# One moving operand for the high and the low part in the first half of two MLPs

## The chip, the cores and the metric

One core of a Trainium2 chip. The metric is the time of one execution on the device in microseconds (us). Here and below TensorE is the matmul engine (PE, its weight loads PEld), VectorE is DVE, ScalarE is ACT, GpSimd is POOL, and SP is the engine that issues most DMAs.

## What is computed

A trunk of two layers over 256 tokens of 1024 features in float32. Layer 0 mixes tokens with differential attention, layer 1 with sparse attention (an indexer picks 64 keys for each query). Each layer ends with the MLP that this case is about:

```
def sq_relu_mlp(h, w1, w2):          # w1: 1024 x 4096, w2: 4096 x 1024
    u = jax.nn.relu(h @ w1)
    return (u * u) @ w2

x = x + mix
x = x + sq_relu_mlp(rms_norm(x, norm_mlp[i]), mlp_w1[i], mlp_w2[i])
```

## The kernel before, in words

**Two parts of each number.** TensorE takes its operands here as float32r, a shorter float32. To keep precision every operand is split: the high part is the value rounded to float32r, the low part the rest. A product a x b is then three products: high x high, high x low, low x high. `unit` loads 1 MB of weights by one DMA on SP's queue into a raw buffer (three of them) and splits it: ScalarE copies to `whi` (L141), VectorE subtracts to `wlo` (L142). There are four pairs of split buffers. Activations lie transposed (features on the partitions, tokens in the columns) as pairs of tiles `act`, each 128 partitions x 4 k-tiles x 256 tokens. `make_h` fills the pair for a norm's output from transposes of x on TensorE (L218, L222, L224).

**The MLP** runs over 8 blocks of 512 hidden columns. `up(b)`, the first half, needs two weight units. For each of four groups of 128 hidden columns (m) it goes over 8 k-tiles of 128 features, with three products of 256 columns each (L464 to L466): a 128 x 128 piece of the weights is the stationary operand, a k-tile of h with its 256 tokens the moving one. All 24 products of a group add up in one half of a PSUM bank, so two groups share a bank and a block takes two banks from the four named `wk`. `post` then evacuates two groups at once (512 columns): ScalarE relu (L471), VectorE the square (L472), ScalarE the square again, rounded to the high part (L475), VectorE the difference as the low part (L476). In block 0 the four groups take a bank each (two `acc`, two `wk`), go over the k-tiles in two turns, and are evacuated one by one. The second half of block b takes two weight units as well: u's pieces are stationary, the weights move in 512 columns, three products each (L146, L148, L150 in the helper `mm3`), added over all blocks in four `acc` banks; after the last block VectorE adds the result to x (L515).

**Order.** The program's order is: up(0), then for each b up(b + 1), the second half of b. The framework's scheduler places instructions on each engine's queue by their dependences and its own estimates, and puts in the waits; a tile is given its buffer when it is first written and gives it back after its last reader. Each engine runs its queue in order. Loads of weights wait for a raw buffer, splits for a pair of split buffers. Lists of pauses (`PAUSE`) order the attention parts by hand; nothing of them lies in the MLPs. `act` has eight buffers of one part each.

Of the kernel before, what the change touches and what calls it, by code (L numbers as in the profile page):

```python
# [9 lines left out]
F32 = mybir.dt.float32  # L10
# [14 lines left out]
# columns of the packed small parameters  # L25
C_NORM = 0            # mix0, mlp0, mix1, mlp1: 8 each
C_GT = 32             # gains after the transposes: diff q, diff k, dsa q, dsa k
C_SUB = 36
C_CQ = 37             # 2
C_ROPE = 40           # 5 x 16  # L30
C_INV = 120           # 8
C_ID = 128            # identity
C_LAM = 256           # q1, k1, q2, k2: 64 each
# [6 lines left out]
# products of the projections that pass before a stage beside them is issued (none if not here)  # L40
# [5 lines left out]
def trunk(ctx: ExitStack, tc: tile.TileContext, x_in, pos_in, pack_in, wf, out):  # L46
# [5 lines left out]
    act = E(tc.tile_pool(name="act", bufs=8))  # L52
# [34 lines left out]
    # products of zeros while the inputs come: the tensor engine's clock rises with use  # L87
# [70 lines left out]
    def rsqrt(ss, parts, shape, scon=None):  # L158
        """(ss * m + eps) ** -0.5 [* scon], parts: (index, m) with m a number or a column;
        a start from exp(-ln / 2) and one step of Newton's method"""  # L160
        v = tiny.tile(shape, F32, name="rs_v")
        y = tiny.tile(shape, F32, name="rs_y")
        a = tiny.tile(shape, F32, name="rs_a")
        r = tiny.tile(shape, F32, name="rs_r", bufs=6)
        with tc.issue_after(tables[0]):
            for i, m in parts:
                nc.vector.tensor_scalar(v[i], ss[i], m, EPS, op0=OP.mult, op1=OP.add)
                nc.scalar.activation(y[i], ss[i], AF.Ln, bias=eps[:, 0:1], scale=m)
            nc.scalar.activation(y, y, AF.Exp, scale=-0.5)
        nc.vector.tensor_tensor(a, y, y, op=OP.mult)  # L170
        nc.vector.scalar_tensor_tensor(a, a, -0.5, v, op0=OP.mult, op1=OP.mult)
        if scon is not None:
            nc.vector.tensor_tensor(y, y, scon, op=OP.mult)
        nc.vector.scalar_tensor_tensor(r, a, 1.5, y, op0=OP.add, op1=OP.mult)
        return r

    def rsqrt_start(v, shape):
        """v ** -0.5 from the exponent's half and three steps, without a table"""
        y = tiny.tile(shape, F32, name="rs_y")
        a = tiny.tile(shape, F32, name="rs_a")  # L180
        nc.vector.tensor_scalar(y.bitcast(I32), v.bitcast(I32), -0.5, float(0x5f3759df),
                                op0=OP.mult, op1=OP.add)
        for _ in range(3):
            nc.vector.tensor_tensor(a, y, y, op=OP.mult)
            nc.vector.scalar_tensor_tensor(a, a, -0.5, v, op0=OP.mult, op1=OP.mult)
            nc.vector.scalar_tensor_tensor(y, a, 1.5, y, op0=OP.add, op1=OP.mult)
        return y

    def row_scale(need_s):
        """mean square of x per token -> 1/(ms+eps) and its square root"""  # L190
        ss = tiny.tile([128, 2], F32, name="rowss")
        for t in range(2):
            j = sc.tile([128, D], F32, name="qn")
            with tc.issue_after(behind[0]):
                nc.scalar.activation(j, x[t], AF.Square, accum_out=ss[:, t:t + 1])
        v = tiny.tile([128, 2], F32, name="rowv")
        nc.vector.tensor_scalar(v, ss, 1.0 / D, EPS, op0=OP.mult, op1=OP.add)
        s2 = tiny.tile([128, 2], F32, name="rows2")
        nc.vector.reciprocal(s2, v)
        s = None  # L200
        if need_s:
            s = const.tile([128, 2], F32, name=f"srow{need_s}")
            nc.vector.tensor_copy(s, rsqrt_start(v, [128, 2]))
        return s, s2

    def new_h():
        return [[act.tile([128, 4, 256], F32R, name="act") for _ in range(2)] for _ in range(2)]
# [3 lines left out]
    def make_h(h, gc, t, n, js=(0, 1)):  # L211
        """columns of x, transposed, with the norm's gain, in two parts"""
        hi, lo = h[n]
# [12 lines left out]
    def lhs(h, kt, t):  # L226
        hi, lo = h[kt // 4]
# [3 lines left out]
    def project(ps, h, parts, n):  # L231
        """ps[t] = h[t] @ w; parts: (columns of a unit's two tiles, number of k-tiles)"""
# [19 lines left out]
    def rope_tables():  # L252
# [20 lines left out]
        # angles beyond 2^23: whole multiples of 2^24 are taken off and reduced by themselves  # L273
# [3 lines left out]
        # multiples of 2 pi, in two parts, times 2 pi in three: the products are exact but the last  # L277
# [11 lines left out]
        # the rest: multiples of 2^24 modulo 2 pi  # L289
# [33 lines left out]
    def rope(v, t, ty, ng, ns, eng):  # L323
        """v: [128, ng*ns, 64] in SBUF; group g has the gains of type ty+g"""
# [17 lines left out]
    def qk_post(ps, m, scon, ty, ng, nq, gcols, nm):  # L342
        """QK-norm, rotary and transposes of 8 heads' columns, ps[t]: [128, 512], the first nq of
        them queries. Keys are scaled here, queries' scales are left to the softmax.
        Returns two tiles [128, 2, 256] (two heads' dims on the partitions, tokens free), scales."""
# [33 lines left out]
    def dots(q, k):  # L379
        """products of two heads' queries and keys, on the two halves of the rows in turn"""  # L380
# [7 lines left out]
    def scores(qT, kT, i, mask):  # L388
        """masked scores of two heads, queries on partitions: columns 0..127 keys of the
        first token tile's queries, 128..383 of the second's. Keys come negated."""  # L390
# [10 lines left out]
    def expo(s, mn, nsc, z):  # L401
        """exp((score - max) * scale), nsc[:, t] = -scale"""
# [16 lines left out]
    def weighted(ps, c, w, aT, v, vc):  # L419
        """ps[:, c + t*w ...] = probabilities @ values"""  # L420
# [4 lines left out]
    def out_proj(o, us, h, gc, needs=((),) * 4):  # L425
        """x += o @ w_out, in four units of two k-tiles; h: the next norm's, transposed;
        needs[u]: the work beside that brings unit u's part of o"""
# [19 lines left out]
    def mlp(h, after):  # L447
# [4 lines left out]
        def up(b):  # L452
            u1 = [unit(pieces=4 if b < 2 else 2) for _ in range(2)]
            uh = act.tile([128, 4, 256], F32R, name="act")
            ul = act.tile([128, 4, 256], F32R, name="act")
# [3 lines left out]
            def group(ps, m, ks):  # L459
                wh, wl = w[m // 2]  # L460
                c = slice((m % 2) * 128, (m % 2) * 128 + 128)
                for k in ks:
                    hh, hl = h[k // 4][0][:, k % 4], h[k // 4][1][:, k % 4]
                    mm(ps, wh[:, k, c], hh, start=k == 0, stop=False)  # L464
                    mm(ps, wh[:, k, c], hl, start=False, stop=False)  # L465
                    mm(ps, wl[:, k, c], hh, start=False, stop=k == 7)  # L466

            def post(ps, m, cnt):
                r = sc.tile([128, 512], F32, name="sq")[:, :cnt * 256]
                q = sc.tile([128, 512], F32, name="on")[:, :cnt * 256]  # L470
                nc.scalar.activation(r, ps, AF.Relu)  # L471
                nc.vector.tensor_tensor(q, r, r, op=OP.mult)  # L472
                oh = uh[:, m:m + cnt].rearrange("p a b -> p (a b)")
                ol = ul[:, m:m + cnt].rearrange("p a b -> p (a b)")
                nc.scalar.activation(oh, r, AF.Square)  # L475
                nc.vector.tensor_tensor(ol, q, oh.bitcast(F32), op=OP.subtract)  # L476

            if b == 0:
                pss = [(acc() if m < 2 else wk())[:, :256] for m in range(4)]
# [3 lines left out]
                for m in range(4):  # L483
                    post(pss[m], m, 1)
            else:
                for mh in range(2):
                    ps = wk()
                    for m in range(2):
                        group(ps[:, m * 256:(m + 1) * 256], mh * 2 + m, range(8))
                    post(ps, mh * 2, 2)  # L490
# [28 lines left out]
    # ================= layer 0: differential attention =================  # L519
# [40 lines left out]
    def diff_probs(ps, res, nm):  # L560
        """unnormalized p1 - lam * p2 of two heads, keys on partitions, and 1 / sums"""
        qT, kT, rs = yield from qk_post(ps, s2c, scon, 0, 2, 4, (C_GT, C_GT + 1), nm)
        zs = tiny.tile([128, 2, 2, 2], F32, name="zs")       # head, component, token tile
# [77 lines left out]
    # ================= layer 1: sparse attention =================  # L641
# [6 lines left out]
    # compressed queries (their scale is left for later), index keys, index weights, index  # L648
    # queries, scores and the choice of the keys
    cqh = act.tile([128, 4, 256], F32R, name="act")  # L650
    cql = act.tile([128, 4, 256], F32R, name="act")
# [95 lines left out]
    # queries, keys, values  # L747
# [22 lines left out]
    def dsa_probs(half, out):  # L770
        """probabilities of eight heads, keys on partitions"""
# [53 lines left out]
def _tiles(w):  # L825
    """[k*128, n] -> [128, k*n]: each partition's k-tiles side by side"""
# [4 lines left out]
def _weights(i):  # L831
    """the weights in the order of their use, [128, columns] blocks one after another"""
# [44 lines left out]
def _pack(i):  # L877
    """small parameters, one column or one row for all partitions each"""
# [40 lines left out]
```

## Time and profile before

| | |
|---|---|
| three timed runs | 614.53 us median, 614.32 to 617.05 |
| profiled execution | span 611.9 us, 9330 instructions; the page gives no other time of it |
| TensorE, products | 597.8 us busy (98%), 3576 |
| TensorE, weight loads | 516.5 us busy (84%), 3576 |
| VectorE | 397.8 us busy (65%), 947 |
| ScalarE | 355.1 us busy (58%), 664 |
| GpSimd | 15.8 us busy (3%), 53 |
| DMA | 102.35 MB, mean 167 GB/s |

One execution was profiled, from the first instruction to the last (the span). A busy time counts each instruction from start to end, so products that overlap in the engine's pipeline count once in the share but have "mean ns" longer than the step from one start to the next; the steps are read from the timeline. "Idle before <-releaser" says what the engine had waited for. A few per cent of the products' records can be missing.

### The profile page before, as it was taken

The numbers are of one execution on the slowest core, as the hardware profiler recorded it, in microseconds if no ns is written. First come the engines' busy times: TensorE is split into PE (matmuls) and PEld (weight loads), VectorE is DVE, ScalarE is ACT, GpSimd is POOL, SyncE is SP. The second block draws the span as 40 slices with busy tenths as digits, with TensorE's granted clock in tenths as the row PEclk, the third lists the DMA queues.
The fourth block names the chain that finished last, engine by engine and source line by source line (L and its number), as shares of the span: only waits on it lengthen the run. The fifth ranks groups of instructions, "written<-read, shape, count | busy, mean of one in ns | idle before, by whom it ended". The sixth has DMA issues, their size and how long they took to land.

```text
span 611.9 us, 9330 instructions
## 1 busy us (share of the span) xinstructions
PE 597.8 (98%) x3576; PEld 516.5 (84%) x3576; DVE 397.8 (65%) x947; ACT 355.1 (58%) x664; POOL 15.8 (3%) x53
## 2 busy tenths in 40 slices
PE   8899999999999999999999899999999999999997
PEld 7677778899989989989887677778999899889986
DVE  5798986577465455456588999766755554564442
ACT  6788987676345345444387589784843453354330
POOL 5400000000000000000000000000000000000000
PEclk9899999999999999999999999999999999999999
DMA  8574343436545545554555226324465565555401
GB/s 312 186 259 154 138 174 127 176 114 227 182 177 205 199 159 193 207 179 153 203 163 182 69 70 207 139 69 138 160 224 177 198 206 168 185 199 197 148 2 69
DMA packets 16029, 102.35 MB, mean 167 GB/s; under 512 B 1904, under 2 KB 2416, under 8 KB 4336
## 3 DMA queue, kind: packets, MB, share of 16 engines
q1 hardware_dynamic: 15696, 101.62, 47.1%
q8 instruction: 28, 0.46, 0.3%
q10 hardware_dynamic: 288, 0.13, 0.1%
q14 instruction: 17, 0.14, 0.1%
HBM read 100.70 MB, written 1.05 MB: 166 GB/s over the span
## 4 chain that ended last, share of the span: by engine, by line
PE 80%; DVE 13%; ACT 2%; POOL 2%; issue 2%; DVEq 0%; POOLq 0%; ACTq 0%
PE acc L150 15%; PE acc L148 15%; PE acc L146 14%; PE wk L466 9%; PE wk L465 9%; PE wk L464 9%; DVE wlo L142 4%; DVE s L396 2%; PE wk L414 2%; PE wk L385 1%; PE wk L218 1%; DVE score L741 1%; DVE qkss L352 1%; ACT whi L141 1%; DVE m L740 1%
## 5 line engine op out<-in xcount | busy, mean ns | idle before, releaser
L142 DVE TENSOR_TENSOR wlo<-raw,whi 128x1024 fp32r<-128x1024 f32 (+2 forms) x210 | 229.8, 1116 | 167.9 <-ACT whi L141 167.8
L141 ACT ACTIVATE whi<-raw 128x1024 fp32r<-128x1024 f32 (+2 forms) x210 | 198.1, 973 | 185.3 <-PE acc L150 90.9
L146 PE MATMUL acc<-whi,act 128*128 128x512 f32 (+1 forms) x504 | 199.8, 397 | 2.0 <-ACT whi L141 2.0
L148 PE MATMUL acc<-wlo,act 128*128 128x512 f32 (+1 forms) x504 | 198.8, 394 | 0.8 <-DVE wlo L142 0.8
L150 PE MATMUL acc<-whi,act 128*128 128x512 f32 (+1 forms) x504 | 198.3, 394 | 0.0
L466 PE MATMUL wk<-act,wlo 128*128 128x256 f32 x480 | 135.9, 283 | 0.0
L465 PE MATMUL wk<-act,whi 128*128 128x256 f32 x480 | 135.9, 283 | 0.0
L464 PE MATMUL wk<-act,whi 128*128 128x256 f32 x480 | 135.8, 283 | 0.0
L146 PEld LDWEIGHTS acc<-whi,act 128*128 128x128 f32 x504 | 95.8, 190 | 21.3 <-ACT whi L141 2.4
L148 PEld LDWEIGHTS acc<-wlo,act 128*128 128x128 f32 x504 | 95.5, 190 | 19.9 <-DVE wlo L142 1.4
L150 PEld LDWEIGHTS acc<-whi,act 128*128 128x128 f32 x504 | 95.6, 190 | 18.9 <-issue 1.0
L464 PEld LDWEIGHTS wk<-act,whi 128*128 128x128 f32 x480 | 92.1, 192 | 0.5
L465 PEld LDWEIGHTS wk<-act,whi 128*128 128x128 f32 x480 | 92.1, 192 | 0.5
L466 PEld LDWEIGHTS wk<-act,wlo 128*128 128x128 f32 x480 | 92.1, 192 | 0.0
L407 ACT ACTIVATE s<-s,nb,rs_r 128x128 f32<-128x128 f32 x64 | 34.2, 537 | 8.0 <-DVE nb L405 8.0
L472 DVE TENSOR_TENSOR on<-sq 128x512 f32<-128x512 f32 (+1 forms) x36 | 22.4, 625 | 1.9 <-ACT sq L471 1.9
L222 ACT ACTIVATE act<-wk,pack 128x128 fp32r<-128x128 f32 x64 | 18.3, 374 | 8.6 <-PE wk L218 8.6
L476 DVE TENSOR_TENSOR act<-on,act 128x512 fp32r<-128x512 f32 (+1 forms) x36 | 22.3, 625 | 0.2
L475 ACT ACTIVATE act<-sq 128x512 fp32r<-128x512 f32 (+1 forms) x36 | 20.7, 574 | 0.1
L224 DVE SCALAR_TENSOR_TENSOR act<-wk,pack,act 128x128 fp32r<-128x128 f32 x64 | 18.0, 343 | 3.7 <-ACT act L222 3.6
L414 PE MATMUL wk<-pack,s 128*128 128x128 f32 x72 | 15.7, 290 | 2.3 <-DVE s L578 1.6
L471 ACT ACTIVATE sq<-wk 128x512 f32<-128x512 f32 (+1 forms) x32 | 17.7, 553 | 0.0
(178 smaller groups left out, 448.6 us busy)
## 6 DMA issues: line engine op xcount, KB each, us to landing
raw<-in_w SPq DMA_DIRECT2D x91, 1024.0 KB, 4.8
x<-in_x SPq DMA_DIRECT2D x4, 256.0 KB, 4.5
raw<-in_w SPq DMA_DIRECT2D x4, 256.0 KB, 5.2
raw<-in_w SPq DMA_DIRECT2D x2, 512.0 KB, 5.5
raw<-in_w SPq DMA_DIRECT2D x1, 984.0 KB, 5.6
raw<-in_w SPq DMA_DIRECT2D x1, 840.0 KB, 4.5
out_dram<-x SPq DMA_DIRECT2D x3, 256.0 KB, 2.0
out_dram<-x SPq DMA_DIRECT2D x2, 128.0 KB, 1.8
```

The lines of the kernel that those rows point to most:

```text
L141: nc.scalar.activation(hi[:, c], raw[:, c], AF.Copy)
L142: nc.vector.tensor_tensor(lo[:, c], raw[:, c], hi[:, c].bitcast(F32), op=OP.subtract)
L146: mm(ps, ah, wh, start=first, stop=False)
L148: mm(ps, ah, wl, start=False, stop=False)
L150: mm(ps, al, wh, start=False, stop=last)
L407: nc.scalar.activation(p[:, TS[t]], s[:, TS[t]], AF.Exp, bias=nb[:, t:t + 1], scale=nsc[:, t:t + 1], accum_out=z[t])
L414: nc.tensor.transpose(pt[:, i * 128:(i + 1) * 128], p[:, i * 128:(i + 1) * 128], ident)
L464: mm(ps, wh[:, k, c], hh, start=k == 0, stop=False)
L465: mm(ps, wh[:, k, c], hl, start=False, stop=False)
L466: mm(ps, wl[:, k, c], hh, start=False, stop=k == 7)
L472: nc.vector.tensor_tensor(q, r, r, op=OP.mult)
L476: nc.vector.tensor_tensor(ol, q, oh.bitcast(F32), op=OP.subtract)
```

## The change

The high and the low part of an activation become the two halves of one tile, and the first half of the MLPs uses them as one moving operand of 512 columns: the weights' high part meets both at once, the bank's first half collects high x high, its second half high x low, and the third product (low weights x high activations) is added to the second half. The evacuation therefore adds the two halves first, and is done for each group of 128 hidden columns by itself. The pool `act` has four buffers of twice the size. Everything else that the diff touches is text: comments are dropped, and other users of the pair take `parts()` or the first two of its three names.

```
-    act = E(tc.tile_pool(name="act", bufs=8))
+    act = E(tc.tile_pool(name="act", bufs=4))
...
+    def parts():
+        a = act.tile([128, 2, 4, 256], F32R, name="act")
+        return a[:, 0], a[:, 1], a
+
     def new_h():
-        return [[act.tile([128, 4, 256], F32R, name="act") for _ in range(2)] for _ in range(2)]
+        return [parts() for _ in range(2)]
...
         def up(b):
             u1 = [unit(pieces=4 if b < 2 else 2) for _ in range(2)]
-            uh = act.tile([128, 4, 256], F32R, name="act")
-            ul = act.tile([128, 4, 256], F32R, name="act")
+            uh, ul, _ = parts()
...
                 for k in ks:
-                    hh, hl = h[k // 4][0][:, k % 4], h[k // 4][1][:, k % 4]
-                    mm(ps, wh[:, k, c], hh, start=k == 0, stop=False)
-                    mm(ps, wh[:, k, c], hl, start=False, stop=False)
-                    mm(ps, wl[:, k, c], hh, start=False, stop=k == 7)
+                    hi, _, both = h[k // 4]
+                    mm(ps.rearrange("p (a b) -> p a b", b=256), wh[:, k, c], both[:, :, k % 4], start=k == 0, stop=False)
+                    mm(ps[:, 256:], wl[:, k, c], hi[:, k % 4], start=False, stop=k == 7)
 
-            def post(ps, m, cnt):
-                r = sc.tile([128, 512], F32, name="sq")[:, :cnt * 256]
-                q = sc.tile([128, 512], F32, name="on")[:, :cnt * 256]
-                nc.scalar.activation(r, ps, AF.Relu)
-                nc.vector.tensor_tensor(q, r, r, op=OP.mult)
-                oh = uh[:, m:m + cnt].rearrange("p a b -> p (a b)")
-                ol = ul[:, m:m + cnt].rearrange("p a b -> p (a b)")
-                nc.scalar.activation(oh, r, AF.Square)
-                nc.vector.tensor_tensor(ol, q, oh.bitcast(F32), op=OP.subtract)
+            def post(ps, m):
+                r = sc.tile([128, 256], F32, name="sq")
+                q = sc.tile([128, 256], F32, name="on")
+                nc.scalar.activation(r, ps[:, 256:], AF.Copy)
+                nc.vector.tensor_tensor(r, ps[:, :256], r, op=OP.add)
+                nc.vector.scalar_tensor_tensor(q, r, 0.0, r, op0=OP.max, op1=OP.mult)
+                nc.scalar.activation(uh[:, m], q, AF.Copy)
+                nc.vector.tensor_tensor(ul[:, m], q, uh[:, m].bitcast(F32), op=OP.subtract)
 
             if b == 0:
-                pss = [(acc() if m < 2 else wk())[:, :256] for m in range(4)]
+                pss = [(acc() if m < 2 else wk()) for m in range(4)]
...
-                    post(pss[m], m, 1)
+                    post(pss[m], m)
             else:
-                for mh in range(2):
+                for m in range(4):
                     ps = wk()
-                    for m in range(2):
-                        group(ps[:, m * 256:(m + 1) * 256], mh * 2 + m, range(8))
-                    post(ps, mh * 2, 2)
+                    group(ps, m, range(8))
+                    post(ps, m)
```

## Rows read from the trace of the kernel before

**Rows 1.** The page: busy time by engine; the chain that ended last.
```profile
PE 597.8 (98%) x3576; PEld 516.5 (84%) x3576; DVE 397.8 (65%) x947; ACT 355.1 (58%) x664; POOL 15.8 (3%) x53
...
PE 80%; DVE 13%; ACT 2%; POOL 2%; issue 2%; DVEq 0%; POOLq 0%; ACTq 0%
```
**Rows 2.** Windows: the two MLPs (start:end, length, busy by engine).
```profile
core 0: us, PE busy (x) PEld busy (x) DVE busy (x) ACT busy (x) POOL busy (x), PEclk, DMA share, GB/s
126.72:308.87 182.15, 182.15 (x1176) 166.27 (x1175) 102.93 (x135) 87.70 (x128) 0.00 (x0) 1.00 0.51 184
428.00:610.90 182.90, 180.21 (x1160) 164.71 (x1158) 95.79 (x119) 79.45 (x110) 0.00 (x0) 1.00 0.47 161
```
**Rows 3.** Waits, the longest in total, of the engines and of SP's queue.
```profile
engine line waited for: us in total, times, longest us
DVE wlo L142 <- ACT whi L141: 167.8, 77, 3.7
ACT whi L141 <- PE acc L150: 90.9, 33, 3.5
ACT whi L141 <- PE wk L465: 87.7, 28, 3.6
...
SPq L135 <- DVE wlo L142: 470.8, 81, 14.7
```
**Rows 4.** Timeline of PE: first products of three blocks (start us, us).
```profile
240.58 0.40 PE L146 MATMUL acc<-whi,act 128*128 128x512 f32 x1
...
251.48 0.28 PE L464 MATMUL wk<-act,whi 128*128 128x256 f32 x1
251.60 0.28 PE L465 MATMUL wk<-act,whi 128*128 128x256 f32 x1
...
263.00 0.40 PE L146 MATMUL acc<-whi,act 128*128 128x512 f32 x1
```
**Rows 5.** Timeline of PE: first and last of 35 products of 328 columns.
```profile
311.38 0.31 PE L148 MATMUL acc<-wlo,act 128*128 128x328 f32 x1
...
316.50 0.31 PE L150 MATMUL acc<-whi,act 128*128 128x328 f32 x1
```
**Rows 6.** Timeline of PE: transposes between products.
```profile
303.49 0.39 PE L218 MATMUL wk<-pack,x 128*128 128x128 f32 x2
303.63 0.48 PE L148 MATMUL acc<-wlo,act 128*128 128x512 f32 x1
303.95 0.39 PE L150 MATMUL acc<-whi,act 128*128 128x512 f32 x1
```
**Rows 7.** Groups of VectorE by shape (busy us, mean ns, idle before).
```profile
L472 DVE TENSOR_TENSOR on<-sq 128x512 f32<-128x512 f32 x28 | 19.2, 684 | 0.0
L476 DVE TENSOR_TENSOR act<-on,act 128x512 fp32r<-128x512 f32 x28 | 19.1, 684 | 0.0
...
L443 DVE TENSOR_TENSOR x<-acc,x 128x256 f32<-128x256 f32 x16 | 5.8, 415 | 0.0
...
L578 DVE SCALAR_TENSOR_TENSOR s<-s,w 128x256 f32<-128x256 f32 x8 | 3.8, 478 | 0.0
...
L472 DVE TENSOR_TENSOR on<-sq 128x256 f32<-128x256 f32 x8 | 3.2, 420 | 1.9 <-ACT sq L471 1.9
L476 DVE TENSOR_TENSOR act<-on,act 128x256 fp32r<-128x256 f32 x8 | 3.2, 418 | 0.2
```
**Rows 8.** Groups of ScalarE by shape.
```profile
L222 ACT ACTIVATE act<-wk,pack 128x128 fp32r<-128x128 f32 x64 | 18.3, 374 | 8.6 <-PE wk L218 8.6
L475 ACT ACTIVATE act<-sq 128x512 fp32r<-128x512 f32 x28 | 17.4, 620 | 0.0
L471 ACT ACTIVATE sq<-wk 128x512 f32<-128x512 f32 x28 | 16.2, 579 | 0.0
...
L475 ACT ACTIVATE act<-sq 128x256 fp32r<-128x256 f32 x8 | 3.3, 412 | 0.1
...
L471 ACT ACTIVATE sq<-wk 128x256 f32<-128x256 f32 x4 | 1.5, 370 | 0.0
```
**Rows 9.** Windows: one period; inside a first-half block; inside a second-half block.
```profile
172.30:194.70 22.40, 22.40 (x146) 20.51 (x146) 11.84 (x12) 10.04 (x12) 0.00 (x0) 1.00 0.51 188
...
140.00:150.00 10.00, 10.00 (x86) 10.00 (x85) 7.87 (x12) 5.37 (x8) 0.00 (x0) 1.00 0.57 210
152.00:161.00 9.00, 9.00 (x41) 7.44 (x41) 5.92 (x6) 4.00 (x6) 0.00 (x0) 1.00 0.50 185
```
**Rows 10.** Timeline of DVE: the low part for the first second-half block.
```profile
141.96 2.35 DVE L142 TENSOR_TENSOR wlo<-raw,whi 128x1024 fp32r<-128x1024 f32 x2
```
**Rows 11.** Timeline of PE: where the first second-half block starts.
```profile
150.90 0.40 PE L146 MATMUL acc<-whi,act 128*128 128x512 f32 x1
151.13 0.40 PE L148 MATMUL acc<-wlo,act 128*128 128x512 f32 x1
```
**Rows 12.** Timeline of PE: the start of layer 0's MLP.
```profile
126.86 0.36 PE L464 MATMUL acc<-act,whi 128*128 128x256 f32 x1
127.06 0.28 PE L465 MATMUL acc<-act,whi 128*128 128x256 f32 x1
127.18 0.38 PE L218 MATMUL wk<-pack,x 128*128 128x128 f32 x2
```
**Rows 13.** Timeline of ACT in the same stretch.
```profile
127.46 2.67 ACT L222 ACTIVATE act<-wk,pack 128x128 fp32r<-128x128 f32 x10
```

More of the change, by code (lines that the diff above doesn't have):

```diff
@@ L204, in row_scale @@
         return s, s2
+    def parts():
+        a = act.tile([128, 2, 4, 256], F32R, name="act")
+        return a[:, 0], a[:, 1], a
     def new_h():
-        return [[act.tile([128, 4, 256], F32R, name="act") for _ in range(2)] for _ in range(2)]
+        return [parts() for _ in range(2)]
     behind = []
     def make_h(h, gc, t, n, js=(0, 1)):
-        hi, lo = h[n]
+        hi, lo, _ = h[n]
         for j in js:
@@ L226, in lhs @@
     def lhs(h, kt, t):
-        hi, lo = h[kt // 4]
+        hi, lo = h[kt // 4][:2]
         c = slice(t * 128, t * 128 + 128)
@@ L646, in trunk @@
             [(*uc[0], 6), (uc[1][0][:, :656], uc[1][1][:, :656], 2)], 328)
-    cqh = act.tile([128, 4, 256], F32R, name="act")
-    cql = act.tile([128, 4, 256], F32R, name="act")
+    cqh, cql, _ = parts()
     cq = [(cqh, cql)]
```

## The prediction

> **What bounds the kernel now.** I read the page first: TensorE is busy 98% of the span and the chain that ended last is 80% TensorE [rows 1]. A busy TensorE need not run at its peak, since its ends are modelled, so I went on to the stretches of the two MLPs. In each, TensorE is busy for all or nearly all of some 182 us at a granted clock of 1.00, its higher level of 2.4 GHz, while VectorE and ScalarE are busy about half of it [rows 2]. The list of waits agrees: its long entries are VectorE waiting for ScalarE's halves of the weights, ScalarE waiting for TensorE to give weight buffers back, and the queue of weight loads waiting for VectorE to free raw buffers [rows 3]. All of them wait, by one or two steps, for TensorE. So an MLP lasts as long as its products take to start one behind another, and the change is worth what it does to those starts.
>
> The timeline gives them. One first-half block (`up` of one b) starts at 251.48 and the second-half products behind it at 263.00: 11.52 us for 96 products of 256 columns, 120.0 ns each. The second-half block before it, 240.58 to 251.48, is 48 products of 512 columns: 227.1 ns each [rows 4]. The difference, 107.1 ns for 256 columns, is 0.418 ns a column, one column per cycle at 2.4 GHz. What is left is 12.9 ns at either width. A third width tests this: the 328-column products start 34 times between 311.38 and 316.50, 150.6 ns apart [rows 5], where 12.9 + 328 x 0.418 gives 150.0. So a product costs its columns and a fixed 13 ns or so, and its weight load lies beside the product ahead of it.
>
> **The change, part by part.** The columns stay: per k-tile and 128 hidden columns 3 x 256 before, 512 + 256 after. One product in three goes, with its weight load: 4 (m) x 8 (k) x 16 (blocks, two layers) = 512 of them. A block has 32 x (227.1 + 120.0) = 11.11 us instead of 11.52, and 16 blocks save 16 x 0.41 = **6.6 us**. All of it is on the path, as nothing else ends later there [rows 2].
>
> That the 512-column product keeps the price of the present one is a choice. Its moving operand is in two runs of 256 columns, 1024 elements apart, which no product before has. Lower end: 13 ns a product lower, as if even its fixed part were hidden, 6.6 us more gain. Upper end: a break in the operand costs what the change from a transpose to a product costs. There a 512-column product holds the engine for 320 ns (303.63 to 303.95) instead of 227, so 93 ns more [rows 6]; 512 x 93 = 47.6 us, a net loss of 41. I take no extra cost: the nearest row is the plain product of the same width, and one third of the products before change to another place in the same tensors at each step without losing the line.
>
> The evacuation grows. Per block before, VectorE has two products and two differences of 512 columns, 4 x 0.684 = 2.74 us; after, four times an addition from PSUM (0.415, as the residual's addition), a maximum-and-product (0.478, as the same form on 256 columns in SBUF) and a difference (0.418): 5.24 us [rows 7]. ScalarE goes from 2 x (0.579 + 0.620) = 2.40 us to 4 x (0.370 + 0.412) = 3.13 us [rows 8]. In one period of 22.40 us (one block of each half) VectorE has 11.84 us of work now and ScalarE 10.04 [rows 9]; after, some 14.3 and 10.8 of 22.0. Cost: nothing, hidden by TensorE. Its cover is this: what a block evacuates is first used a second-half block later, 10.9 us on, and the chain of five operations takes 2.1 us. Behind these operations in VectorE's and ScalarE's queues wait the splits of the weights, and behind those, by raw buffers, the weight DMAs on SP's queue. Where the two engines are fullest, at the start of an MLP, the low part of the weights for the first second-half block is split by 144.31 [rows 10] and its first reader, the second product of that block, starts at 151.13 [rows 11]: 6.8 us to spare. The first block's evacuation adds 5.24 - 4 x (0.420 + 0.418) = 1.9 us and half of the second's 1.3 us more. Over 3 us remain. If that cover were gone, the loss would be the overhang, once per layer.
>
> PSUM: a later block now takes four banks (one per m) instead of two. Four are there and the same bank comes round a period later, so no wait. The four banks of the first block are as many as before.
>
> The merged tile of high and low part is one buffer of four in place of two of eight; what is alive at once (h, two hidden blocks; o and h) is the same number of bytes, and pairs were freed within one product of each other. Cost nothing. One new wait is possible at the start of each MLP. There the first products (126.86) start while the last transposes of x are still to be evacuated [rows 12, 13]: already the tile in use is being written in other columns. The joint read spans from the high to the low part. If that is taken as one stretch, the first product waits for the tile's last high part, the second piece of the group that starts at 127.46, so until about 128.2 (pieces of 0.37, some 0.27 apart). Five products of 120 ns that now run between the transposes come later: 0.6 us a layer, 1.2 in all. Lower end 0: only what is read is waited for. I take 0.3. Queued behind it on TensorE are the remaining transposes, on which the rest of h waits.
>
> **Sum.** Profiled span 611.9 - 6.6 + 0.3 = 605.6 us. The page gives no time of that execution beyond its span; the median of the timed runs is 614.5, 2.6 more, for what lies around it. That stays: **608.2 us**.
>
> At one place a page speaks against the size. The Trainium skill (TensorE: Matmul & The Clock Gate, Back-to-back issue gap) has a warm product cost its columns at 2.4 GHz plus 2.5 ns, not 13. By that 512 products fewer save 1.3 us, an estimate from that page, and the time would be 613.2. The rows give 120.0 ns for 256 columns where the page's form gives 109, so the measurement decides on the size of the fixed part. That all of it goes with the instruction no row shows.
>
> **The rivals.**
> 1. The fixed part, or most of it, stays with the run of columns and not with the instruction: two runs in one product cost twice 12.9. For it: no operand in two runs is in the trace. Against: nothing in the rows speaks of runs. Gain nil, plus 0.3: 614.8. (The case of the page above is near it.)
> 2. Slower: the break in the moving operand stalls the array. Place: every 512-column product of the first half; from 12.9 ns a break on there is no gain, from 19 ns on (another 3.1 us) it is slower by over 0.5%. Priced by the switch row, 93 ns: 614.5 + 41 = 655. Against: rows 4 and 5 show the line of columns undisturbed by any change of address between products.
> 3. The weight loads pace the first half. For it: there PEld is busy 10.00 of 10.00 us, in the second half 7.44 of 9.00 [rows 9]. Then the remaining 256-column product, its load beside a 512-column one, would fall to its columns, 107.1 ns, and the pair to 334.2: 512 x (360 - 334.2) = 13.2 us, 601.3. Against: the 328- and 512-column products have the same 13 ns with their loads well hidden.
>
>    The Trainium skill (Perfetto Trace Analysis, Identifying the Most-Contended Engine) would have TensorE judged by this share of loads; the three widths on one line say otherwise here.
> 4. The gain is there, but about three us come back: the wait at the MLPs' start at its upper end (1.2), and a split that is late at the start of an MLP, held in its queue behind an evacuation that waits for its group of products. A group lasts 11.11 / 4 = 2.8 us and over 3 us are spare, so it takes two such holds; their overhang is some 1 us a layer. Against: the splits there are ahead of need by more than any one hold. 608.2 + 0.9 + 2 = 611.1.
>
> **How the numbers follow.** Forecast 0.70 (its own range 607 to 609.5), rival 4 0.13, rival 1 0.09, rival 2 0.05, rival 3 0.03. The range of 8 in 10 takes in the forecast and rival 4: 606.0 to 612.5. Half a per cent, about what a measurement of this kernel can tell from no change, is 3.1 us: faster means under 611.4. The forecast, rival 3 and some two thirds of rival 4 are there: 0.82. Rival 1 and the rest of rival 4 are within: 0.13. Rival 2 is slower: 0.05.
>
> **What would show it.** In a first-half block of the changed kernel, starts 227 and 120 ns apart in turn and 11.1 us from the first to the second half's next product; an MLP of some 179 us; 512 products and loads fewer; TensorE still without idle time in the MLPs; VectorE at 65% there. A step of 240 ns or more after the 512-column products would be rival 1 (above 246, rival 2), one of 107 after the others rival 3. Idle time of TensorE released by `wlo`, or by `act` at the start of an MLP, would be rival 4. The prediction is wrong if the steps are right and the time isn't: then the attention parts, which the diff leaves alone, have moved.

## The result and the profile after

Eight runs of each kernel: 612.0 us median (609.86 to 612.57) against 614.7 (614.22 to 617.27). The ratio of the changed kernel to the one before is 0.994, 95% interval 0.9922 to 0.9959, or 2.5 to 4.8 us less. The forecast was 608.2, 1.0% less. The direction held and so did the wide range; the likeliest case's own range, 607 to 609.5, did not. One run of the kernel before and one of `wides`, both in a later comparison, took 3.34 ms each; the ratios below are without them. The profiled execution's span is 609.2 us, 2.7 less than before.

The page of the changed kernel, its line of busy time by engine:

```profile
PE 595.2 (98%) x3064; PEld 490.0 (80%) x3064; DVE 428.7 (70%) x1067; ACT 368.5 (60%) x720; POOL 15.9 (3%) x53
```

512 products and 512 weight loads are gone, as worked out, VectorE and ScalarE are fuller, and TensorE is as busy as it was [rows 1]. The windows of the two MLPs and of one period, which answer to [rows 2, 9] (start:end, length, busy by engine, granted clock):

```profile
126.88:307.06 180.18, 180.18 (x920) 152.09 (x919) 118.19 (x194) 94.25 (x156) 0.00 (x0) 1.00 0.52 186
426.90:608.20 181.30, 178.67 (x907) 151.18 (x905) 111.47 (x180) 86.23 (x138) 0.00 (x0) 1.00 0.47 163
183.27:205.50 22.23, 22.23 (x113) 18.80 (x112) 13.91 (x20) 11.02 (x16) 0.00 (x0) 1.00 0.53 191
```

TensorE has no idle time in the MLPs, and VectorE is at 63% of a period. But the period is 22.23 us where 22.0 was expected. The timeline of PE for one first-half block of the changed kernel, its first two products, some in its middle, and the first one behind it:

```profile
183.27 0.39 PE L469 MATMUL wk<-act,whi 128*128 128x512 f32 x1
183.50 0.28 PE L470 MATMUL wk<-act,wlo 128*128 128x256 f32 x1
...
191.03 0.40 PE L469 MATMUL wk<-act,whi 128*128 128x512 f32 x1
191.26 0.28 PE L470 MATMUL wk<-act,wlo 128*128 128x256 f32 x1
191.38 0.40 PE L469 MATMUL wk<-act,whi 128*128 128x512 f32 x1
191.62 0.28 PE L470 MATMUL wk<-act,wlo 128*128 128x256 f32 x1
191.74 0.40 PE L469 MATMUL wk<-act,whi 128*128 128x512 f32 x1
191.98 0.28 PE L470 MATMUL wk<-act,wlo 128*128 128x256 f32 x1
192.09 0.40 PE L469 MATMUL wk<-act,whi 128*128 128x512 f32 x1
...
194.56 0.40 PE L146 MATMUL acc<-whi,act 128*128 128x512 f32 x1
```

From 183.27 to 194.56 there are 32 pairs of a wide (512) and a narrow (256) product: 11.29 us, 352.8 ns a pair, not 347.1. The steps repeat every three pairs, 191.03 to 192.09 = 1.06 us, with wide steps of 230 to 240 ns and narrow ones of 110 to 120. Blocks 2 to 7 of both layers have this length to 0.01 us. Blocks 0 and 1 are faster in this execution. From the first pair behind the transposes of layer 0 to the first product of the second half there are 30 pairs in 10.40 us:

```profile
139.73 0.39 PE L469 MATMUL wk<-act,whi 128*128 128x512 f32 x1
...
150.13 0.39 PE L146 MATMUL acc<-whi,act 128*128 128x512 f32 x1
```

That is 346.7 ns a pair, the forecast's price, in a pattern of two pairs (693 ns); the expectations below call it 345. So the same products in the same order step in one of two ways.

Where the 2.7 us lie, by the starts of the same products in the two traces:

| stretch | before | after | difference |
|---|---|---|---|
| to the first product of layer 0's MLP | 126.86 | 126.88 | +0.02 |
| layer 0's MLP, to the first 328-column product | 182.01 | 180.17 | -1.84 |
| layer 1's attention, to its MLP's first product | 118.79 | 119.86 | +1.07 |
| layer 1's MLP, to the last product | 180.16 | 178.27 | -1.89 |
| end | 4.08 | 4.02 | -0.06 |

Two things are to be explained: the MLPs gave 3.7 us and not 6.6, and the attention of layer 1, whose instructions are in the same order, took 1.07 us more. The latter first, by the timeline of PE there:

```profile
347.42 0.41 PE L374 MATMUL wk<-pack,qn 128*128 128x128 f32 x2 [2.17 <-DVE qn L345]
...
348.66 0.63 PE L148 MATMUL acc<-wlo,act 128*128 128x512 f32 x1
349.09 0.63 PE L150 MATMUL acc<-whi,act 128*128 128x512 f32 x1
```

and the window of its slow stretch:

```profile
348.00:351.40 3.40, 3.40 (x10) 2.65 (x9) 3.40 (x15) 2.93 (x4) 0.00 (x0) 0.50 0.02 5
```

After 2.17 us idle, in which TensorE waited for VectorE's rotary step, the granted clock is 0.50, the lower level of 1.2 GHz, and 512-column products step by 430 ns instead of 227. The kernel before idles at the same place, as long, and keeps 1.00 there:

```profile
349.22 0.41 PE L369 MATMUL wk<-pack,qn 128*128 128x128 f32 x2 [2.17 <-DVE qn L340]
...
349.40:353.00 3.60, 3.60 (x21) 2.90 (x20) 3.60 (x14) 2.87 (x4) 0.00 (x0) 1.00 0.00 0
```

The price, some 1.1 us, is not one of the change's instructions.

### The profile page after: what moved, and what is told of

It is laid out like the page before. It is cut to its first block, busy times and chain, and to the rows that moved or that the text cites. A ratio compares the mean times of both kernels' runs of the same rounds, so it can differ in the third digit from the quotient of the medians.

```text
span 609.2 us, 8462 instructions
## 1 busy us (share of the span) xinstructions
PE 595.2 (98%) x3064; PEld 490.0 (80%) x3064; DVE 428.7 (70%) x1067; ACT 368.5 (60%) x720; POOL 15.9 (3%) x53
## 4 chain that ended last, share of the span: by engine, by line
PE 82%; DVE 10%; ACT 3%; POOL 2%; issue 2%; DVEq 0%; POOLq 0%; ACTq 0%
PE wk L469 18%; PE acc L150 15%; PE acc L148 15%; PE acc L146 15%; PE wk L470 9%; DVE wlo L142 4%; DVE s L401 2%; PE wk L419 2%; PE acc L469 1%; PE wk L390 1%; PE wk L223 1%; ACT whi L141 1%; PE wk L374 1%; PE acc L470 1%; DVE score L742 1%
## 5 line engine op out<-in xcount | busy, mean ns | idle before, releaser
L469 PE MATMUL wk<-act,whi 128*128 128x512 f32 x480 | 169.5, 397 | 0.0
L469 PEld LDWEIGHTS wk<-act,whi 128*128 128x128 f32 x480 | 90.1, 188 | 21.9
L470 PEld LDWEIGHTS wk<-act,wlo 128*128 128x128 f32 x480 | 90.6, 189 | 0.5
L478 ACT ACTIVATE act<-on 128x256 fp32r<-128x256 f32 x64 | 26.3, 416 | 57.6 <-DVE on L477 57.6
L479 DVE TENSOR_TENSOR act<-on,act 128x256 fp32r<-128x256 f32 x64 | 26.7, 423 | 14.5 <-ACT act L478 12.7
L475 ACT ACTIVATE sq<-wk 128x256 f32<-128x256 f32 x60 | 22.4, 375 | 17.5 <-PE wk L470 17.5
L477 DVE SCALAR_TENSOR_TENSOR on<-sq 128x256 f32<-128x256 f32 x64 | 26.6, 420 | 0.9
L476 DVE TENSOR_TENSOR sq<-wk,sq 128x256 f32<-128x256 f32 x60 | 24.8, 417 | 0.0
L517 DVE SCALAR_TENSOR_TENSOR x<-acc,rows,x 128x256 f32<-128x256 f32 x16 | 7.0, 479 | 15.1 <-PE acc L150 15.1
```

The lines of the kernel that those rows point to most:

```text
L469: mm(ps.rearrange("p (a b) -> p a b", b=256), wh[:, k, c], both[:, :, k % 4], start=k == 0, stop=False)
L470: mm(ps[:, 256:], wl[:, k, c], hi[:, k % 4], start=False, stop=k == 7)
L477: nc.vector.scalar_tensor_tensor(q, r, 0.0, r, op0=OP.max, op1=OP.mult)
L478: nc.scalar.activation(uh[:, m], q, AF.Copy)
L479: nc.vector.tensor_tensor(ul[:, m], q, uh[:, m].bitcast(F32), op=OP.subtract)
```

## The experiments

The theories: (1) pairs of a wide and a narrow product fall into one of two step patterns by the way a block is entered; (2) the break in the wide product's operand costs 6 to 8 ns (the mechanism of the prediction's first rival); (3) the larger evacuation takes part of the gain; and later (A) a product costs its columns plus a fixed 13 ns, with something for a change of width, against (B) narrow products wait for their weight loads.

**contig.** The MLPs' input with high and low part of a k-tile side by side:

```
+    def side_by_side():
+        a = act.tile([128, 4, 2, 256], F32R, name="act")
+        return a[:, :, 0], a[:, :, 1], a
...
-                    mm(ps.rearrange("p (a b) -> p a b", b=256), wh[:, k, c], both[:, :, k % 4], start=k == 0, stop=False)
+                    mm(ps, wh[:, k, c], both[:, k % 4].rearrange("p a b -> p (a b)"), start=k == 0, stop=False)
...
-    h = new_h()
+    h = new_h(side_by_side)
```

> The activations of the MLPs' input are laid out so that a k-tile's high and low part are 512 neighbouring columns: the wide product has one run of columns in place of two, all else as in the changed kernel. Theory 1 (the pairs of a 512- and a 256-column product fall into one of two repeating patterns, 345 or 353 ns a pair, by the way the block is entered): the steps stay as they are, 353 ns a pair in blocks 2 to 7 of both layers, 345 in blocks 0 and 1; time within 1 us of the changed kernel, 612. Theory 2 (the break in the operand costs the 6 to 8 ns): every block 345 to 347 ns a pair, 11.05 us a block, 12 blocks x 0.24 = 2.9 us less, 609.

Ratio to before 0.9921, interval 0.9906 to 0.9936, 611.09 us. The window of block 3 of layer 0, from its first product to the one behind it:

```profile
184.04:195.33 11.29, 11.29 (x66) 9.81 (x65) 7.79 (x13) 6.32 (x10) 0.00 (x0) 1.00 0.51 184
```

11.29 us, as with two runs. Theory 2 falls: the break costs nothing. Blocks 0 and 1 were expected at 345 ns a pair; together they took 0.4 us longer than in the changed kernel in both layers and stepped at 353, so the faster pattern is not theirs by right.

**split.** For seven of eight k-tiles the wide product in two narrow ones:

```
-                    mm(ps.rearrange("p (a b) -> p a b", b=256), wh[:, k, c], both[:, :, k % 4], start=k == 0, stop=False)
+                    if k == 0:
+                        mm(ps.rearrange("p (a b) -> p a b", b=256), wh[:, k, c], both[:, :, k % 4], start=True, stop=False)
+                    else:
+                        mm(ps[:, :256], wh[:, k, c], hi[:, k % 4], start=False, stop=False)
+                        mm(ps[:, 256:], wh[:, k, c], both[:, 1, k % 4], start=False, stop=False)
                     mm(ps[:, 256:], wl[:, k, c], hi[:, k % 4], start=False, stop=k == 7)
```

> As the changed kernel, but for 7 of 8 k-tiles the wide product is issued as two products of 256 columns, into the same two halves of the bank: new layout and new evacuation, nearly the old products. If the evacuation and the layout cost nothing (theories 1 and 2), blocks take 28 x 360 + 4 x 347 = 11.47 us, the MLPs are 16 x 0.04 = 0.6 us shorter than before, and the time is 614, against 614.6 before. If the evacuation costs on the path (theory 3: VectorE's 1.9 us more per block takes part of the gain), it is above 616. Of the half-level clock after the idle gap of layer 1: if the place of the gap in time decides, this kernel, whose gap lies within half a us of the one before, keeps the full clock there.

Ratio 0.9999, interval 0.998 to 1.0017. The window of one block:

```profile
184.52:195.99 11.47, 11.47 (x93) 11.29 (x92) 7.89 (x13) 6.32 (x10) 0.00 (x0) 1.00 0.50 184
```

11.47 us, as expected, with all of the new evacuation in it. The two MLPs together take 0.6 us less than before, as expected, so layout and evacuation cost nothing on the path, theory 3 falls, and the whole gain is the wide product's. The median, 615.3 us, missed the 614 expected; the interval takes in both. The clock fell after the gap here too (349.5 to 353.0 by the records), against the expectation.

**entries.** Another order of the same products in blocks 2 to 6 (`wide` and `cross` issue the wide and the narrow product of a k-tile, `halves` three narrow ones):

```
+                if b == 2 and m == 0:
+                    order = [(wide, 0), (cross, 0), (halves, 1)] + [(f, k) for k in range(2, 8) for f in (wide, cross)]
+                elif b == 3:
+                    order = [(wide, 0), (cross, 0)] + [(f, k) for k in range(1, 7) for f in (cross, wide)] + [(wide, 7), (cross, 7)]
+                elif b == 4:
+                    order = [(wide, k) for k in range(8)] + [(cross, k) for k in range(8)]
+                elif b == 5:
+                    order = [(f, k) for j in range(4) for f in (wide, cross) for k in (2 * j, 2 * j + 1)]
+                elif b == 6:
+                    order = [(f, k) for j in range(2) for f in (wide, cross) for k in range(4 * j, 4 * j + 4)]
...
```

> The changed kernel with another order of the same products in some blocks; blocks 0, 1 and 7 as they are. Block 2: the second k-tile of its first group in three 256-column products. Block 3: from the second k-tile on the 256-column product first. Block 4: per group eight wide products, then eight narrow. Block 5: two wide, two narrow in turn. Block 6: four and four. Theory 1: the pattern can be moved, some of blocks 2 to 6 fall to 345 to 347 ns a pair, alike in both layers, block 7 stays at 353. Theory 2 (each wide product costs 6 to 8 ns for its break): blocks 2 to 6 stay at 352 to 354 a pair, whatever the order. In theory 1 block 4 is 8 x 227 + 8 x 120 = 2776 a group, 347 a pair, plus what the change between widths costs.

Blocks 2 to 7 take 11.30, 11.23, 11.15, 11.14, 11.20 and 11.29 us, the same in both layers to 0.01. The timeline of PE in block 4, eight wide and eight narrow in turn (merged, xcount):

```profile
207.22 1.98 PE L468 MATMUL wk<-act,whi 128*128 128x512 f32 x8
209.03 1.12 PE L471 MATMUL wk<-act,wlo 128*128 128x256 f32 x8
209.98 2.00 PE L468 MATMUL wk<-act,whi 128*128 128x512 f32 x8
211.82 1.11 PE L471 MATMUL wk<-act,wlo 128*128 128x256 f32 x8
...
218.36 0.40 PE L146 MATMUL acc<-whi,act 128*128 128x512 f32 x1
```

The first eight wide products, which follow wide ones, take 1.81 us, 226 ns each; the next eight, which follow narrow ones, 1.84, 230 each. Block 2, entered differently, goes on at 353. So the loss depends on how the widths are mixed, and none of these entries moved it: theory 2 falls once more, and of theory 1 there remains that there are two patterns, without what chooses between them. The loss does not follow the number of changes: four and four (11.20) has fewer than two and two (11.14) and loses more. What makes a wide product late beside narrow ones was open.

**widths.** Runs of products that nobody reads, behind the last block:

```
+    def row(n, m, i):
+        mm(ps[:m, :n], W[i % 8][:, :m], flat[:, :n], start=True, stop=True)
...
+    for n, m in ((256, 128), (256, 64), (384, 128), (128, 128), (192, 128)):
+        sep()
+        for i in range(40):
+            row(n if i % 2 else 512, m, i)
...
```

> The changed kernel, and behind its last block runs of products that nobody reads, all from one tile of activations: 40 each of 128, 192 and 256 columns, of 256 columns with a stationary operand of 64 columns instead of 128, of 384; then 512 columns in turn with 256, with 256 (64 stationary columns for both), with 384, 128 and 192. Between the runs 16 of 512. Theory A (a product costs its columns and 13 ns, and a change between wide and narrow costs a few ns more): 66, 93, 120, 120 and 173 ns for the runs of one width; the 64 stationary columns change nothing. Theory B (a narrow product waits for its weights, which are loaded beside the product ahead, so that a 256-column product is paced by its 128-column load): 128, 192 and 256 columns all step at 113 to 120 ns; with 64 stationary columns 256 steps at 107 to 110; in turn with 512 the pair with 256 is 353 ns as in the changed kernel, and with 64 stationary columns some 335 to 340; the pair of 512 and 384 is 400, without extra; those of 512 and 192 or 128 are above 227 + 93 and 227 + 66 by 20 ns and more.

The timeline of PE: L834 are the runs of 40 (of those in turn, the row names the first product's shape), L831 the 16 products between; "128*64" has 64 stationary columns, and so 64 rows of output:

```profile
610.99 4.58 PE L834 MATMUL acc<-act 128*128 128x128 f32 x40
615.40 3.90 PE L831 MATMUL acc<-act 128*128 128x512 f32 x16
619.14 4.61 PE L834 MATMUL acc<-act 128*128 128x192 f32 x40
623.59 3.82 PE L831 MATMUL acc<-act 128*128 128x512 f32 x16
627.25 4.96 PE L834 MATMUL acc<-act 128*128 128x256 f32 x40
632.04 3.82 PE L831 MATMUL acc<-act 128*128 128x512 f32 x16
635.69 4.71 PE L834 MATMUL acc<-act 128*64 128x256 f32 x40
640.23 3.81 PE L831 MATMUL acc<-act 128*128 128x512 f32 x16
643.89 7.12 PE L834 MATMUL acc<-act 128*128 128x384 f32 x40
650.85 3.83 PE L831 MATMUL acc<-act 128*128 128x512 f32 x16
654.51 7.21 PE L834 MATMUL acc<-act 128*128 128x512 f32 x40
661.56 3.85 PE L831 MATMUL acc<-act 128*128 128x512 f32 x16
665.25 6.99 PE L834 MATMUL acc<-act 128*64 128x512 f32 x40
672.08 3.80 PE L831 MATMUL acc<-act 128*128 128x512 f32 x16
675.71 8.29 PE L834 MATMUL acc<-act 128*128 128x512 f32 x40
683.84 3.80 PE L831 MATMUL acc<-act 128*128 128x512 f32 x16
687.47 6.91 PE L834 MATMUL acc<-act 128*128 128x512 f32 x40
694.22 3.87 PE L831 MATMUL acc<-act 128*128 128x512 f32 x16
697.93 6.93 PE L834 MATMUL acc<-act 128*128 128x512 f32 x40
704.71 3.82 PE L831 MATMUL acc<-act 128*128 128x512 f32 x16
```

From a run's start to the next one's, divided by its products:

| run | ns a product | run | ns a pair |
|---|---|---|---|
| 128 columns | 110 | 512 and 256 | 353 |
| 192 | 111 | 512 and 256, 64 stationary columns | 342 |
| 256 | 120 | 512 and 384 | 407 |
| 256, 64 stationary columns | 114 | 512 and 128 | 338 |
| 384 | 174 | 512 and 192 | 339 |

Theory A wanted 66 ns for 128 columns; the step stays at 110, and pairs with 128 and 192 columns cost the same 338 or so. That fits theory B: a narrow product adds no less than some 110 ns to the stream (227 + 111 in these pairs), which by this theory is the time of its 128-column load. No run had so narrow a product with a short load, so that the floor is the load's own time is inferred, not shown. The Trainium skill (TensorE: Matmul & The Clock Gate, LDWEIGHTS (loading the stationary operand)) gives a load its columns divided by 1.2 in ns, 107 for 128 columns; the measured floor of 110 agrees within 3%. The records of the loads don't show it: they last 190 ns, 134 with 64 columns, and neighbouring ones overlap.

By the starts of single products in the trace the wide one begins only 60 ns behind a 128-column one, but what follows it comes 280 ns later and not 227; by this reading the wide one waits for its weights behind its recorded start. At 256 columns the two are close: the product alone, with a short load, takes 114, with the full load 120, and in turn with a wide one the pair loses 11 ns (353 against 342). By single starts its wide product steps by 236 ns and its narrow one by 117; with the short load by 227 and 113, which is no loss. The run changes load and output rows together, so it shows their sum. The pair of 353 ns is that of the changed kernel, here with other data and at another place.

Theory B had 400 for the pair with 384; it took 407, so products in turn with 384 columns are late as well, which the load's 110 ns alone doesn't explain. Its figures for 64 stationary columns were a little low too (107 to 110 where 114 was measured, 335 to 340 for the pair of 342). Nor does it say why the same pair steps at 346.7 ns in blocks 0 and 1 of some executions.

**again, twotwo, wides.** The changed kernel once more, and two orders with fewer changes of width. `twotwo` has the two wide products of two k-tiles, then their two narrow ones:

```
-                for k in ks:
...
+                for k0 in ks[::2]:
+                    for k in (k0, k0 + 1):
+                        mm(ps.rearrange("p (a b) -> p a b", b=256), wh[:, k, c], h[k // 4][2][:, :, k % 4], start=k == 0, stop=False)
+                    for k in (k0, k0 + 1):
+                        mm(ps[:, 256:], wl[:, k, c], h[k // 4][0][:, k % 4], start=False, stop=k == 7)
```

`wides` has all wide products of a block, then all narrow ones:

```
...
+                pss = [wk() for _ in range(4)]
+                for m in range(4):
+                    group(pss[m], m, range(8), True, False)
+                for m in range(4):
+                    group(pss[m], m, range(8), False, True)
+                    post(pss[m], m)
```

> The changed kernel once more, for the comparison on one chip with the two others of this call: 0.992 to 0.996 of the kernel before; blocks 2 to 7 at 11.29 us. All theories say the same.

> The changed kernel with two wide products, then the two narrow ones of the same k-tiles, in all blocks: half as many changes between widths. If the changes cost what was lost: 11.14 us a block in place of 11.29 (11.41 for the mean of blocks 0 and 1 with their transposes goes down alike), 16 x 0.15 = 2.4 us less than the changed kernel, ratio to before 0.989 to 0.991. If each wide product costs its 6 ns wherever it stands: no difference to the changed kernel.

> The changed kernel with all 32 wide products of a block first, then all 32 narrow ones (block 0 in two turns); the four groups are evacuated within the last 4 us of the block. If the changes between widths cost what was lost: 32 x 226.7 + 32 x 120.0 and one change, 11.10 to 11.12 us a block, 16 x 0.18 = 2.8 us less than the changed kernel, ratio 0.988 to 0.990. If the evacuation, now in one lump of 5.2 us of VectorE behind the block, comes on the path, TensorE waits for act or wlo in the second half and the gain is gone.

| kernel | ratio to before | interval | median us | blocks 2 to 7, us |
|---|---|---|---|---|
| again | 0.9935 | 0.9915 to 0.9955 | 611.07 | 11.29 |
| twotwo | 0.9893 | 0.9873 to 0.9913 | 608.31 | 11.14 |
| wides | 0.9888 | 0.9867 to 0.991 | 608.17 | 11.09 |

The timeline of PE in `wides`, one block:

```profile
161.48 0.39 PE L470 MATMUL wk<-act,whi 128*128 128x512 f32 x1
...
168.74 0.64 PE L472 MATMUL wk<-act,wlo 128*128 128x256 f32 x4
...
172.57 0.40 PE L146 MATMUL acc<-whi,act 128*128 128x512 f32 x1
```

32 wide products in 7.26 us, 227 ns each, 32 narrow ones in 3.83, 120 each: the prices that the prediction took from the trace before, and 11.09 us where it had 11.11. Both orders beat both kernels, and by what the MLPs save: together they take 6.05 us (`twotwo`) and 6.25 us (`wides`) less than in the kernel before, of the 6.6 forecast. The lump of evacuation behind the block stays hidden: TensorE waits for neither `act` nor `wlo` in the MLPs.

**fill.** Four products that nobody reads, ahead of the transposes in the idle gap of layer 1:

```
+            if nm == "k0" and t == 0:
+                fill = wk()
+                mm(fill[:, :48], ident, qn[:, 0, 16:64], start=True, stop=True)
+                for n in range(3):
+                    mm(fill[:, :384], ident, cmask, start=True, stop=True)
```

> The changed kernel with four more products, which nobody reads, in TensorE's idle gap of 2.2 us in layer 1's attention (345.2 to 347.4, ahead of the first transposes of the keys). Theory: the half-level clock from 348.0 to 351.4 in the changed kernel follows that gap; the gap filled, the clock stays at 2.4 GHz there, the products after it keep 227 ns instead of 430, and the span is some 1.1 us shorter, 608.1, the time 611. Rival: the clock falls for another reason (it fell in one profiled execution by chance): the stretch at half level is still there or the time does not move; 612.

614.25 us, ratio 0.9979, interval 0.9963 to 0.9995: slower than the changed kernel. The clock kept its upper level behind the gap, but TensorE idled 1.86 us ahead of the filling products, and layer 1's attention (the third stretch of the table above) takes 120.6 us against 118.7 in `entries`, which has no filling and kept its clock as well. Why it is longer stays open. The run decides nothing about the clock. Of the nine other profiles the clock fell behind the gap in five (the changed kernel, `again`, `split`, `twotwo`, `widths`) and not in four (before, `contig`, `entries`, `wides`), with about the same gap in all. The attention takes 119.8 to 119.9 us where it fell and 118.7 to 118.8 where it did not: 1.1 us. What decides stays open. The timed runs differ in the clock too: of 23 runs of the kernel before in this comparison, eleven had a mean granted clock of 0.991 and took 615.0 to 617.1 us, and the two with 0.999 took 612.96 and 613.42. So the ratios carry some of its luck, and the lengths of blocks 2 to 7, which ran at 1.00, are the firmer evidence.

## Why the prediction was half right

- **What bounds it: right.** The MLPs last as long as the steps between products. `split`, whose MLPs are 0.6 us shorter, as the prices of its products alone give it, shows that nothing else of the change is on the path.
- **512 products fewer, the columns the same: right.** The counts are those of the page.
- **"The 512-column product keeps the price of the present one", and the narrow one too: the step that failed.** The pair costs 352.8 ns, not 347.1: in 12 blocks of 32 pairs 2.2 us. The second-half products behind a block start late as well, 10.94 us a block in place of 10.91, another 0.5 us over both layers. Of 6.6 us some 3.9 remain; the MLPs gave 1.84 + 1.89 = 3.7. Where blocks 0 and 1 fell into the slower pattern as well, in one layer (`again`) or in both (`contig`), they gave 3.4 and 3.0.
- **Why it failed.** "A product costs its columns and a fixed 13 ns or so, and its weight load lies beside the product ahead of it" was read from runs of one width, three points on a line. `widths` adds the points that leave it: at 128 columns 110 ns, where the line has 66. At 256 columns 6 of the 13 ns go with the short load (114 against 120), so there the fixed part was not all fixed. That products in turn cost more than the sum of their runs is shown (353 against 347), and so is that the loss vanishes with the short load and its fewer output rows; that the wide product waits for its load is inferred, and why the pair of 347 ns occurs as well stays open. The third rival named the loads; it had the pair fall to 334 with them, and it came out above the forecast's 347. The prediction set aside what the Trainium skill (Perfetto Trace Analysis, Identifying the Most-Contended Engine) says of judging TensorE by the share of its loads, since three widths lie on one line; `widths` shows that the line ends at narrow products, which theory B has paced by their loads; by that reading the rule pointed at the right place, though it gives no price.
- **The break in the operand costs nothing: right,** by `contig`.
- **Evacuation hidden: right,** by `split` (VectorE 63% of a period, 65% forecast).
- **The wait at the MLPs' start: there is none.** The first product starts at 126.88 against 126.86 [rows 12]; the 0.3 us taken for it were not spent.
- **Not foreseen:** the clock at the gap in layer 1. In the profiled execution it took back 1.1 us of the 3.8 that the other stretches gave.

The range was wide enough for a loss of the size of the fourth rival, but by none of its mechanisms: that 612.0 lies within 606.0 to 612.5 is luck, as the lost steps and the clock were in no rival at these prices.

## What to carry to other kernels

Before two widths of product are mixed, measure them in turn, above all where one is so narrow that its weight load may pace it: a fixed cost read from runs of one width need not carry over to an alternation. Where a wide product replaces two narrow ones and a narrow one stays, issue like widths together; here all the wide ones of a block first gave back all of the lost steps (11.09 us a block), for a change of loop order. And when a change moves work in time, read the granted clock of every stretch before a difference in an untouched part is put down to the change.

## What the runs showed of the hardware

- With a 128-column float32r weight load ahead of each, a narrow product adds no less than some 110 ns to the stream: in runs of one width 110 (128 columns) and 111 (192), and in turn with 512 columns, whose step alone is 227, the pair takes 338 and 339 (`widths`).
- 512- and 256-column products in turn settle in a pattern that repeats every three pairs, 1060 ns; a pattern of two pairs in 693 ns, without loss, was seen in blocks 0 and 1 of some executions (both layers of the changed kernel, one of the two in `again` and in `widths`).
- A moving operand in two runs of 256 columns streams like one of 512 (`contig`).
